# Attention scores of a two-layer decoder: one PSUM bank per head, and the keys' low parts multiplied by the queries' high parts alone in half of the array's rows

## The chip, the core and the metric

The kernel runs on one core of a Trainium2 chip. The core has five engines with an instruction queue each: TensorE (PE in the profile, its weight loads PEld), VectorE (DVE), ScalarE (ACT), GpSimd (POOL) and SyncE (SP, which here only issues DMAs). TensorE multiplies a stationary operand, loaded into its 128x128 array, with a moving operand, and writes to PSUM, which has eight banks; DVE and ACT read PSUM, POOL does not. The metric is the device time of one execution in microseconds (us).

## What is computed

The reference has two layers on x of 256 positions by 2048 channels: a retention and short-convolution mixer, then sliding-window attention. The change touches the attention scores of the second layer alone:

```python
def swa_sinks(q, k, v, sinks):          # 32 query heads, 4 key heads, head width 64
    ...                                 # blocks of 128 queries, n = 2 blocks
    scores = jnp.einsum('bnihgd,bnjhd->bnhgij', qb, kk) * (d ** -0.5)
    band = (kj <= qi) & (qi - kj < WINDOW)           # WINDOW = 128
    scores = jnp.where(valid, scores, -1e30)
    m = jnp.maximum(jnp.max(scores, axis=-1, keepdims=True), sink)
    p = jnp.exp(scores - m)
    p = p / (jnp.sum(p, axis=-1, keepdims=True) + jnp.exp(sink - m))
    return jnp.einsum('bnhgij,bnjhd->bnihgd', p, vv)
```

Query block 0 sees key block 0 under a causal mask. Query block 1 sees, for each key position, either the key of block 0 or the one of block 1: the window is exactly one block long, so of the two products at one position just one is valid, and the kernel picks between them by a triangular mask.

## The kernel before

**Products in three terms.** Every fp32 matrix is split into a high part (rounded to the type that TensorE reads at full rate, fp32r) and a low part, the rest. The four big projections are computed as high x high + high x low + low x high. Weights come in pieces of 512 KB (`Chunk.split`, L156): a DMA, an ACT copy that rounds to the high part (`wh`, L164), a DVE subtraction that leaves the low part (`wl`, L165). A piece feeds 12 matmuls of 128x128 by 128x512 (L142); `wh` and `wl` have five buffers each. Eight pieces make a chunk of 512 output columns.

**Small work between the pieces.** Attention is a generator that is advanced one step after each piece (`feed` calls `step`, L131 to 135), so that its small matmuls stand between the 12 matmuls of one piece and those of the next. The odd layer's chunks alternate queries and gates (`ODD_KIND`), for four groups g of eight heads, one key head each. The instructions go to each engine's queue in an order that a scheduler makes from the program; every engine then works through its queue strictly in that order.

**A group's steps.** `turn_q` transposes the rotated queries into `qT` (names q1T in the profile): for a pair of heads, the even head's high part stands in partitions 0 to 63 and its low part in 64 to 127, the odd head's the other way round. `kT` holds the keys twice, in both halves of the partitions, as high parts (index 0) and low parts (index 1). Then `scores(j, h)` (L608) is called four times per group, j = 0, 1 and h = 0, 2, each time for two heads: 16 calls in all. After two calls `shift(j)` (L630) makes the exponents' offsets `nm` and the sinks' terms `es`; `exponentials` (L645) takes the exponential of a 128x128 tile per head and query block on ACT, in place in `pr`, summing into `den`; `turn_p` (L677) transposes four such tiles into a PSUM tile `pt`, which ACT copies to `ph` (L685) and DVE subtracts into `pl` (L686); `turn_gate` (L667) transposes the gate into `gt`; `values` multiplies with the values into `ov`.

**PSUM.** The pool `at` has two banks, for score tiles and `ov` in turn, and `tp` has two banks, for all transposes (`pt`, `gt`, `qt`) in turn. A tile can be written only when the readers of the tile two before it in its pool are done.

**One call of scores before.** Six matmuls with 256 moving columns each: for each head of the pair one for query block 0 (L613, moving operand: high and low keys of block 0 side by side, into the first bank) and two for query block 1 (L615 with the high keys of both blocks, L616 with the low ones, added up in the second bank). The stationary operand has 128 rows, high and low parts of the query, so all four products are formed, low x low as well. ACT copies the first half of bank one for both heads (L618), DVE adds the other half (L619), adds the mask and takes the maximum per head (L621); ACT copies half of bank two (L626), DVE overwrites the places of the other key block by `copy_predicated` (L627) and takes maxima (L628).

Of the kernel before, what the change touches and what calls it, by code (L numbers as in the profile page):

```python
# [8 lines left out]
F32 = mybir.dt.float32  # L9
F32R = mybir.dt.float32r  # L10
AF = mybir.ActivationFunctionType
ALU = mybir.AluOpType
# [3 lines left out]
P = 128  # L16
D = 2048
S = 256
# [7 lines left out]
HD = 64  # L26
# [13 lines left out]
C_AMASK = C_ID + 128  # L40
C_LOWER = C_AMASK + P
# [16 lines left out]
def hybrid_kernel(  # L58
# [13 lines left out]
    nc = tc.nc  # L72
# [7 lines left out]
    at = ctx.enter_context(tc.tile_pool(name="at", bufs=2, space=PSUM))  # L80

    cst = cp.tile([P, C_END], F32, tag="cst", name="cst")
# [383 lines left out]
    op = ctx.enter_context(tc.tile_pool(name="o", bufs=1))  # L466
# [21 lines left out]
    kT = op.tile([P, 4, T, 2, P], F32R, tag="kT", name="kT")  # L488
# [1 line left out]

    vs = op.tile([P, 3, 4, 2, HD], F32R, tag="vs", name="vs")
    act2 = Act("a2")
    lower = cst[:, C_LOWER : C_LOWER + P].bitcast(mybir.dt.uint32).unsqueeze(1).broadcast_to([P, 2, P])

    def work(name, shape, dt=F32):
        return tw.tile(shape, dt, tag="w2", name=name)
# [89 lines left out]
    def attention(g, rr, rs, qs):  # L586
        ah, al = act2.new()
        qT = op2.tile([P, 4, 2, T, P], F32R, tag="qT", name=f"q1T{g}", bufs=1)
# [18 lines left out]

        def scores(j, h):  # L608

            s0 = at.tile([P, 2, 2, P], F32, tag="at", name=f"s0{g}{j}{h}")  # L610
            s1 = at.tile([P, 2, S], F32, tag="at", name=f"s1{g}{j}{h}")
            for i in range(2):
                nc.tensor.matmul(s0[:, i], qT[:, 2 * j + h // 2, i, 0, :], kT[:, g, 0], start=True, stop=True)  # L613
            for i in range(2):
                nc.tensor.matmul(s1[:, i], qT[:, 2 * j + h // 2, i, 1, :], kT[:, g, :, 0, :], start=True, stop=False)  # L615
                nc.tensor.matmul(s1[:, i], qT[:, 2 * j + h // 2, i, 1, :], kT[:, g, :, 1, :], start=False, stop=True)  # L616
            p0, p1 = pr[j][:, h : h + 2, 0, :], pr[j][:, h : h + 2, 1, :]
            nc.scalar.activation(p0, s0[:, :, 0, :], AF.Copy)  # L618
            nc.vector.tensor_tensor(out=p0, in0=s0[:, :, 1, :], in1=p0, op=ALU.add)  # L619
            for i in range(2):  # L620
                nc.vector.tensor_tensor_reduce(  # L621
                    out=p0[:, i], in0=p0[:, i], in1=cst[:, C_AMASK : C_AMASK + P], scale=1.0, scalar=-3.0e38,
                    op0=ALU.add, op1=ALU.max, accum_out=mx[j][:, 0, h + i : h + i + 1],
                )

            nc.scalar.activation(p1, s1[:, :, 0:P], AF.Copy)  # L626
            nc.vector.copy_predicated(p1, lower, s1[:, :, P:S])  # L627
            nc.vector.tensor_reduce(out=mx[j][:, 1, h : h + 2], in_=p1, axis=AX.X, op=ALU.max)  # L628

        def shift(j):  # L630
# [88 lines left out]
        for t in range(T):  # L719
            nc.vector.tensor_scalar(  # L720
                out=rr[:, t, :], in0=rs[t], scalar1=r1[:, t : t + 1], scalar2=HD ** -0.5, op0=ALU.mult, op1=ALU.mult
# [9 lines left out]
        for j in range(2):  # L731
            mx[j] = op2.tile([P, T, 4], F32, tag="mx", name=f"mx{g}{j}")
            pr[j] = op2.tile([P, 4, T, P], F32, tag="pr", name=f"pr{g}{j}")
            scores(j, 0)
            if j:
                exponentials(0, 0)
            yield
            scores(j, 2)
            shift(j)
            if j:  # L740
                exponentials(0, 1)
                divisor(0)
            yield
# [72 lines left out]
    for t in range(T):  # L816
# [3 lines left out]
        for c in range(1 + t):  # L820
            n = slice(c * N // (1 + t), (c + 1) * N // (1 + t))
# [84 lines left out]
```

## Time and profile before

| what | value |
|---|---|
| runs shown, median (lowest to highest) | 794.79 us (793.71 to 795.48), 3 runs |
| profiled execution, its own time | 795.05 us |
| its span, first to last instruction | 793.1 us |
| busy share PE, DVE, ACT, POOL | 99%, 64%, 52%, 6% |
| calls of scores in the span | 16, from 534.6 to 704.7 us |
| matmuls of scores | 96, of 3620 |

The busy share of an engine is an average over the span. A matmul's duration in the records holds its way through the array, so the pace of PE is read from the starts of successive instructions rather than from durations. Times of rows are microseconds from the span's start. A row of the timeline gives start, length, engine, line, operation, output and inputs, shapes and how often; a bracket tells how long the engine was idle before and who ended that.

### The profile page before, as it was taken

The page shows a single profiled execution, that of the slowest core. Times are in us where ns is not written, and L with a number is a line of the kernel's source. Part 1 is how long each engine was busy: PE and PEld are TensorE (multiplying, and loading weights), DVE is VectorE, ACT ScalarE, POOL GpSimd, SP SyncE. Part 2 cuts the span into 40 slices and gives each one's busy share as a digit, 9 for nine tenths or more (in the row PEclk, how much of TensorE's full clock was granted, in tenths as well). Part 3 has the DMA queues.
Part 4 walks back from the last instruction along what each step waited for, and adds up shares of the span by engine and source line. Part 5 has one row for each costly group of instructions (what it writes and reads, how often), then busy time and mean ns, then how long its engine had stood idle before and what let it go on. Part 6 is the DMA issues. An engine that isn't in the chain of part 4 may idle for free.

```text
span 793.1 us, 9901 instructions
## 1 busy us (share of the span) xinstructions
PE 786.6 (99%) x3620; PEld 651.5 (82%) x3620; DVE 505.9 (64%) x759; ACT 414.1 (52%) x645; POOL 45.0 (6%) x45
## 2 busy tenths in 40 slices
PE   8999999999999999999999999999999999999998
PEld 6888888888888888888888888888888888888886
DVE  6666454664445466545857664797998887977651
ACT  6743434444443434343435444658758678686431
POOL 0000000000000000000000000210300301301000
PEclk9999999999999999999999999999999999999999
DMA  8966645555456555556555555463464464445750
GB/s 311 394 241 230 201 145 186 184 183 191 134 188 201 194 185 186 187 186 206 167 198 172 186 186 189 156 213 107 159 213 130 140 209 159 156 138 185 233 166 26
DMA packets 41375, 147.09 MB, mean 185 GB/s; under 512 B 4720, under 2 KB 5360, under 8 KB 41072
## 3 DMA queue, kind: packets, MB, share of 16 engines
q1 hardware_dynamic: 40896, 146.21, 55.0%
q8 instruction: 28, 0.46, 0.2%
q10 hardware_dynamic: 432, 0.27, 0.1%
q14 instruction: 19, 0.16, 0.1%
HBM read 144.36 MB, written 2.10 MB: 185 GB/s over the span
## 4 chain that ended last, share of the span: by engine, by line
PE 99%; DMA 1%; ACT 0%; DVE 0%; ACTq 0%; DVEq 0%; issue 0%
PE pse L142 44%; PE psoq L142 11%; PE psoo L142 11%; PE psog L142 11%; PE pseo L142 11%; PE psokv L142 3%; PE pt L681 1%; PE ov L704 1%; PE ov L703 1%; DMA xt<-in_xt 1%; PE s L613 0%; PE s L616 0%; PE s L615 0%; PE gt L672 0%; PE qt L598 0%; PE rt L284 0%
## 5 line engine op out<-in xcount | busy, mean ns | idle before, releaser
L165 DVE TENSOR_TENSOR wle<-we,whe 128x1024 fp32r<-128x1024 f32 (+1 forms) x129 | 156.4, 1217 | 147.9 <-ACT whe L164 147.7
L164 ACT ACTIVATE whe<-we 128x1024 fp32r<-128x1024 f32 (+1 forms) x129 | 135.4, 1052 | 173.1 <-PE pse L142 158.8
L142 PE MATMUL pse<-whe,a0h 128*128 128x512 f32 x512 | 200.1, 396 | 1.3 <-ACT whe L164 1.3
L142 PE MATMUL pse<-whe,a0l 128*128 128x512 f32 x512 | 198.4, 391 | 0.0
L142 PE MATMUL pse<-wle,a0h 128*128 128x512 f32 x512 | 197.6, 390 | 0.0
L142 PEld LDWEIGHTS pse<-whe,a0h 128*128 128x128 f32 x512 | 96.6, 189 | 22.4 <-ACT whe L164 2.9
L142 PEld LDWEIGHTS pse<-whe,a0l 128*128 128x128 f32 x512 | 96.7, 189 | 20.3
L142 PEld LDWEIGHTS pse<-wle,a0h 128*128 128x128 f32 x512 | 96.3, 188 | 19.5
L164 ACT ACTIVATE wheo<-weo 128x1024 fp32r<-128x1024 f32 x32 | 33.9, 1061 | 48.2 <-PE pseo L142 32.7
L165 DVE TENSOR_TENSOR wleo<-weo,wheo 128x1024 fp32r<-128x1024 f32 x32 | 39.2, 1225 | 27.5 <-ACT wheo L164 27.5
L164 ACT ACTIVATE whoo<-woo 128x1024 fp32r<-128x1024 f32 x32 | 33.9, 1062 | 40.3 <-PE psoo L142 32.7
L165 DVE TENSOR_TENSOR wloo<-woo,whoo 128x1024 fp32r<-128x1024 f32 x32 | 38.9, 1224 | 24.8 <-ACT whoo L164 24.4
L164 ACT ACTIVATE whoq<-woq 128x1024 fp32r<-128x1024 f32 x32 | 34.0, 1062 | 35.3 <-PE psoq L142 14.3
L142 PE MATMUL psog<-whog,a1h 128*128 128x512 f32 x128 | 51.1, 400 | 0.0
L142 PE MATMUL psoq<-whoq,a1h 128*128 128x512 f32 x128 | 50.9, 398 | 0.0
L142 PE MATMUL pseo<-wheo,c0h 128*128 128x512 f32 x128 | 50.8, 397 | 0.0
L142 PE MATMUL psoo<-whoo,a2h 128*128 128x512 f32 x128 | 50.3, 393 | 0.0
L142 PE MATMUL psoo<-whoo,a2l 128*128 128x512 f32 x128 | 50.1, 391 | 0.0
L142 PE MATMUL psog<-whog,a1l 128*128 128x512 f32 x128 | 50.0, 391 | 0.0
L142 PE MATMUL psoq<-wloq,a1h 128*128 128x512 f32 x128 | 50.0, 391 | 0.0
L142 PE MATMUL psoq<-whoq,a1l 128*128 128x512 f32 x128 | 50.0, 391 | 0.0
L142 PE MATMUL pseo<-wheo,c0l 128*128 128x512 f32 x128 | 50.0, 391 | 0.0
(177 smaller groups left out, 1209.4 us busy)
## 6 DMA issues: line engine op xcount, KB each, us to landing
we<-in_w SPq DMA_DIRECT2D x127, 512.0 KB, 3.3
weo<-in_w SPq DMA_DIRECT2D x32, 512.0 KB, 3.3
woq<-in_w SPq DMA_DIRECT2D x32, 512.0 KB, 4.4
wog<-in_w SPq DMA_DIRECT2D x32, 512.0 KB, 3.3
woo<-in_w SPq DMA_DIRECT2D x32, 512.0 KB, 4.3
wokv<-in_w SPq DMA_DIRECT2D x8, 512.0 KB, 3.3
x<-in_xr SPq DMA_DIRECT2D x2, 1024.0 KB, 8.5
out_y<-y SPq DMA_DIRECT2D x7, 256.0 KB, 4.2
```

The source lines that it names most:

```text
L142: nc.tensor.matmul(self.ps[t], self.act(kt)[a][:, t * P : (t + 1) * P], w[:, k * N : (k + 1) * N], start=self.n[t] == 1, stop=self.n[t] == ...
L164: nc.scalar.activation(wh[:, ws], raw[:, ws], AF.Copy)
L165: nc.vector.tensor_tensor(out=wl[:, ws], in0=raw[:, ws], in1=f32(wh[:, ws]), op=ALU.subtract)
L681: nc.tensor.transpose(tr[:, h, :], pr[j][:, h, t, :], ident)
L703: nc.tensor.matmul(of, v, ph, start=first, stop=False)
L704: nc.tensor.matmul(of, v, pl, start=False, stop=last)
```

## The change

`scores` is rewritten. Each head of the pair has a bank of its own, `sc[i]`, with three blocks of 128 columns: block 0 for query block 0, blocks 1 and 2 for query block 1 against the two key blocks. Per head, two matmuls use all 128 rows (high and low queries by high keys: 128 and 256 moving columns, L615). Then four matmuls add the low keys, and they take only the 64 partitions that hold the head's high queries, 0 to 63 for the even head and 64 to 127 for the odd one, alternating (128, 128, 256, 256 columns, L622). The product of low queries with low keys is left out. The ACT copy and the DVE addition of query block 0 go; the mask and maximum read PSUM directly (L628); the ACT copy and the predicated copy of query block 1 are now one per head (L634, L635).

```diff
-    lower = cst[...].bitcast(mybir.dt.uint32).unsqueeze(1).broadcast_to([P, 2, P])
+    lower = cst[...].bitcast(mybir.dt.uint32)
...
-            s0 = at.tile([P, 2, 2, P], F32, tag="at", name=f"s0{g}{j}{h}")
-            s1 = at.tile([P, 2, S], F32, tag="at", name=f"s1{g}{j}{h}")
+            sc = [at.tile([P, 3, P], F32, tag="at", name=f"s{g}{j}{h}{i}") for i in range(2)]
             for i in range(2):
-                nc.tensor.matmul(s0[:, i], qT[:, 2 * j + h // 2, i, 0, :], kT[:, g, 0], start=True, stop=True)
-            for i in range(2):
-                nc.tensor.matmul(s1[:, i], qT[:, 2 * j + h // 2, i, 1, :], kT[:, g, :, 0, :], start=True, stop=False)
-                nc.tensor.matmul(s1[:, i], qT[:, 2 * j + h // 2, i, 1, :], kT[:, g, :, 1, :], start=False, stop=True)
+                for t, n in ((0, slice(0, 1)), (1, slice(1, 3))):
+                    k = kT[:, g, : t + 1, 0, :]
+                    nc.tensor.matmul(
+                        sc[i][:, n], qT[:, 2 * j + h // 2, i, t, :], k, start=t == 0, stop=False, skip_group_check=True
+                    )
+
+            for t, n in ((0, slice(0, 1)), (1, slice(1, 3))):
+                for i in range(2):
+                    e = slice(i * HD, (i + 1) * HD)
+                    nc.tensor.matmul(
+                        sc[i][:, n], qT[e, 2 * j + h // 2, i, t, :], kT[e, g, : t + 1, 1, :],
+                        start=False, stop=True, skip_group_check=True,
+                    )
-            nc.scalar.activation(p0, s0[:, :, 0, :], AF.Copy)
-            nc.vector.tensor_tensor(out=p0, in0=s0[:, :, 1, :], in1=p0, op=ALU.add)
             for i in range(2):
                 nc.vector.tensor_tensor_reduce(
-                    out=p0[:, i], in0=p0[:, i], in1=cst[:, C_AMASK : C_AMASK + P], ...
+                    out=p0[:, i], in0=sc[i][:, 0], in1=cst[:, C_AMASK : C_AMASK + P], ...
                 )
-            nc.scalar.activation(p1, s1[:, :, 0:P], AF.Copy)
-            nc.vector.copy_predicated(p1, lower, s1[:, :, P:S])
+            for i in range(2):
+                nc.scalar.activation(p1[:, i], sc[i][:, 1], AF.Copy)
+                nc.vector.copy_predicated(p1[:, i], lower, sc[i][:, 2])
```

Lines behind `scores` stand eight further down in the changed file (the exponentials are L648 before and L656 now, `pl` is L686 before and L694 now).

The queues change with it, beyond `scores` itself. First **PE, the fourth call of group 1**, before (s_4798 and s_4799 are the call's two score tiles, q1T the queries):

```order
L142 MATMUL psoq_1_4699<-whoq_2_4781,a1l_3201 128x512
L613 MATMUL s_4798<-kT,q1T_4563 128x256 x2
L615 MATMUL s_4799<-kT,q1T_4563 128x256
L616 MATMUL s_4799<-kT,q1T_4563 128x256
L615 MATMUL s_4799<-kT,q1T_4563 128x256
L616 MATMUL s_4799<-kT,q1T_4563 128x256
```

and now:

```order
L142 MATMUL psoq_1_4709<-whoq_2_4795,a1l_3201 128x512
L615 MATMUL s_4812<-kT,q1T_4571 128x128
L615 MATMUL s_4812<-kT,q1T_4571 128x256
L615 MATMUL s_4813<-kT,q1T_4571 128x128
L615 MATMUL s_4813<-kT,q1T_4571 128x256
L622 MATMUL s_4812<-kT,q1T_4571 128x128
L622 MATMUL s_4813<-kT,q1T_4571 128x128
L622 MATMUL s_4812<-kT,q1T_4571 128x256
L622 MATMUL s_4813<-kT,q1T_4571 128x256
```

Six matmuls become eight at the same place; the first needs the first bank and the third needs the second bank, where before the first two needed one bank and the next four the other.

Then **ACT, from the third call of group 1 to behind the fourth**, before (L618 and L626 copy score tiles, L648 are exponentials of the first two calls' scores, L643 the sinks' exponential, L164 the rounding of a weight piece):

```order
L164 ACTIVATE whoq_6_4935<-woq_6_4934 128x1024
L643 ACTIVATE es_4734<-es_4734 128x8
L618 ACTIVATE pr_4760<-s_4761 128x2x128
L626 ACTIVATE pr_4760<-s_4762 128x2x128
L648 ACTIVATE pr_4677,den_4735<-pr_4677,nm_4733,rr_4457 128x128 x5
L618 ACTIVATE pr_4760<-s_4798 128x2x128
L626 ACTIVATE pr_4760<-s_4799 128x2x128
L648 ACTIVATE pr_4677,den_4735<-pr_4677,nm_4733,rr_4457 128x128 x3
L164 ACTIVATE whoq_7_4965<-woq_7_4964 128x1024
```

and now (L634 are the copies, L656 the exponentials):

```order
L164 ACTIVATE whoq_6_4951<-woq_6_4950 128x1024
L651 ACTIVATE es_4746<-es_4746 128x8
L656 ACTIVATE pr_4685,den_4747<-pr_4685,nm_4745,rr_4465 128x128 x4
L634 ACTIVATE pr_4772<-s_4773 128x128
L634 ACTIVATE pr_4772<-s_4774 128x128
L656 ACTIVATE pr_4685,den_4747<-pr_4685,nm_4745,rr_4465 128x128 x4
L164 ACTIVATE whoq_7_4981<-woq_7_4980 128x1024
L634 ACTIVATE pr_4772<-s_4812 128x128
```

Four exponentials now stand ahead of the third call's copies, and the other four and a weight piece ahead of the fourth call's. Groups 2 and 3 have the same rows; in group 0 one exponential stands ahead of the third call's copies.

Last **DVE, behind the fourth call of group 1**, before (L165 are weight pieces, pl_4854 is the low part of the first transposed tile pt_4848):

```order
L663 TENSOR_TENSOR gv_4693<-gv_4693,den_4735 128x2x256
L165 TENSOR_TENSOR wloq_7_4966<-woq_7_4964,whoq_7_4965 128x1024
L686 TENSOR_TENSOR pl_4854<-pt_4848,ph_4853 128x512
L686 TENSOR_TENSOR pl_4886<-pt_4880,ph_4885 128x512
L655 TENSOR_TENSOR den_4815<-den_4815,es_4814 128x8
```

and now (L635 are the fourth call's predicated copies, L636 its maxima, L647 to L650 `shift`, pl_4870 the low part of the first transposed tile):

```order
L165 TENSOR_TENSOR wloq_7_4982<-woq_7_4980,whoq_7_4981 128x1024
L635 COPY_PREDICATED pr_4772<-cst,s_4812 128x128
L635 COPY_PREDICATED pr_4772<-cst,s_4813 128x128
L671 TENSOR_TENSOR gv_4703<-gv_4703,den_4747 128x2x256
L636 TENSOR_REDUCE mx_4771<-pr_4772 128x2
L647 TENSOR_TENSOR mx_4771<-mx_4771,rr_4465 128x8
L648 TENSOR_TENSOR mx_4771<-mx_4771,sml 128x8
L165 TENSOR_TENSOR wlog_0_5061<-wog_0_5059,whog_0_5060 128x1024
L649 TENSOR_SCALAR nm_4829<-mx_4771 128x8
L650 TENSOR_TENSOR es_4830<-sml,mx_4771 128x8
L694 TENSOR_TENSOR pl_4870<-pt_4864,ph_4869 128x512
```

The first low part `pl` stood right behind the piece wloq_7; now the fourth call's copies and maxima, the gate's scaling and the next piece wlog_0 stand between the two. Groups 2 and 3 again have the same rows; in group 0 `pl` still follows wloq_7.

More of the change, by code (lines that the diff above doesn't have):

```diff
@@ L492, in hybrid_kernel @@
     act2 = Act("a2")
-    lower = cst[:, C_LOWER : C_LOWER + P].bitcast(mybir.dt.uint32).unsqueeze(1).broadcast_to([P, 2, P])
+    lower = cst[:, C_LOWER : C_LOWER + P].bitcast(mybir.dt.uint32)
     def work(name, shape, dt=F32):
@@ L608, in scores @@
         def scores(j, h):
-            s0 = at.tile([P, 2, 2, P], F32, tag="at", name=f"s0{g}{j}{h}")
-            s1 = at.tile([P, 2, S], F32, tag="at", name=f"s1{g}{j}{h}")
+            sc = [at.tile([P, 3, P], F32, tag="at", name=f"s{g}{j}{h}{i}") for i in range(2)]
             for i in range(2):
-                nc.tensor.matmul(s0[:, i], qT[:, 2 * j + h // 2, i, 0, :], kT[:, g, 0], start=True, stop=True)
-            for i in range(2):
-                nc.tensor.matmul(s1[:, i], qT[:, 2 * j + h // 2, i, 1, :], kT[:, g, :, 0, :], start=True, stop=False)
-                nc.tensor.matmul(s1[:, i], qT[:, 2 * j + h // 2, i, 1, :], kT[:, g, :, 1, :], start=False, stop=True)
+                for t, n in ((0, slice(0, 1)), (1, slice(1, 3))):
[10 more added lines that the diff above has]
+                    )
             p0, p1 = pr[j][:, h : h + 2, 0, :], pr[j][:, h : h + 2, 1, :]
-            nc.scalar.activation(p0, s0[:, :, 0, :], AF.Copy)
-            nc.vector.tensor_tensor(out=p0, in0=s0[:, :, 1, :], in1=p0, op=ALU.add)
             for i in range(2):
                 nc.vector.tensor_tensor_reduce(
-                    out=p0[:, i], in0=p0[:, i], in1=cst[:, C_AMASK : C_AMASK + P], scale=1.0, scalar=-3.0e38,
+                    out=p0[:, i], in0=sc[i][:, 0], in1=cst[:, C_AMASK : C_AMASK + P], scale=1.0, scalar=-3.0e38,
                     op0=ALU.add, op1=ALU.max, accum_out=mx[j][:, 0, h + i : h + i + 1],
                 )
-            nc.scalar.activation(p1, s1[:, :, 0:P], AF.Copy)
-            nc.vector.copy_predicated(p1, lower, s1[:, :, P:S])
+            for i in range(2):
+                nc.scalar.activation(p1[:, i], sc[i][:, 1], AF.Copy)
+                nc.vector.copy_predicated(p1[:, i], lower, sc[i][:, 2])
             nc.vector.tensor_reduce(out=mx[j][:, 1, h : h + 2], in_=p1, axis=AX.X, op=ALU.max)
```

## The prediction

> **What bounds the kernel now.** I read the busy shares first, then the chain that ended last, then PE's list of waits.
>
> ```profile
> PE 786.6 (99%) x3620; PEld 651.5 (82%) x3620; DVE 505.9 (64%) x759; ACT 414.1 (52%) x645; POOL 45.0 (6%) x45
> ...
> PE 99%; DMA 1%; ACT 0%; DVE 0%; ACTq 0%; DVEq 0%; issue 0%
> ...
> PE warm L199 <- DVE zero L196: 1.5, 1, 1.5
> PE pse L142 <- ACT whe L164: 1.3, 1, 1.3
> ```
>
> PE is busy for 99% of the span, is 99% of the chain, and its matmuls waited only twice, both times at the program's start. So the end is set by the pace of PE's queue: whatever lengthens one of its rows, or makes one of its rows wait, is paid in full, and work taken from DVE or ACT is worth nothing by itself. PE's pace at the fourth call of group 1 and behind it:
>
> ```profile
> 597.90 0.39 PE L142 MATMUL psoq<-whoq,a1l 128*128 128x512 f32 x1
> 598.13 0.40 PE L613 MATMUL s<-kT,q1T 128*128 128x256 f32 x2
> 598.36 0.28 PE L615 MATMUL s<-kT,q1T 128*128 128x256 f32 x1
> 598.48 0.28 PE L616 MATMUL s<-kT,q1T 128*128 128x256 f32 x1
> 598.60 0.28 PE L615 MATMUL s<-kT,q1T 128*128 128x256 f32 x1
> 598.72 0.28 PE L616 MATMUL s<-kT,q1T 128*128 128x256 f32 x1
> 598.84 0.40 PE L142 MATMUL psoq<-whoq,a1h 128*128 128x512 f32 x1
> ...
> 601.59 0.60 PE L681 MATMUL pt<-cst,pr 128*128 128x128 f32 x4
> ...
> 604.80 0.60 PE L681 MATMUL pt<-cst,pr 128*128 128x128 f32 x4
> 605.24 0.60 PE L672 MATMUL gt<-cst,gv 128*128 128x128 f32 x4
> ```
>
> From start to start a 512-column matmul takes 0.23 us (597.90 to 598.13) and a 256-column one 0.12. A call takes 598.84 - 598.13 = 0.71, the 12 matmuls behind it 2.75, and the next call is due 3.46 after the last.
>
> **Term one: the call's own length on PE.** Six rows of 256 columns go, eight come: four with all rows of the array (128, 256, 128, 256 columns), four with half of the rows (128, 128, 256, 256). The trace has no fp32r matmul of 128 columns, none in half the rows, and no two that ran side by side. The nearest rows are the retention's:
>
> ```profile
> 100.58 0.63 PEld L299 LDWEIGHTS rsc<-qT,kT 128*128 128x128 f32 x4
> ...
> 100.79 0.61 PE L299 MATMUL rsc<-qT,kT 128*128 128x128 f32 x4
> 101.24 1.03 PE L295 MATMUL rsc<-qT,kT 128*128 128x256 f32 x4
> ```
>
> Four 128-column matmuls with a weight load each took 101.24 - 100.79 = 0.45, so 0.11 each; that is fp32, which streams slower, so it is the upper end. The lower end is the line through 0.23 and 0.12, which gives 0.07. The four full rows then take between 2 x 0.07 + 2 x 0.12 = 0.38 and 0.46. The four half rows take 0.19 if the two heads' halves run side by side, and up to 0.46 if they run in turn. Without a price for going from full to half rows and back the call lies between 0.56 and 0.92. For that price no row exists. Nothing speaks for a gain from it, so its lower end is zero; the upper end is an empty array and a load that is not hidden: 0.28 - 0.12 = 0.16 of tail (598.36 row) plus a 0.19 load (PEld rows below), 0.35 per switch, 0.70 per call. So a call takes 0.56 to 1.62. I take 0.92, no overlap and no price of switching: it is the row nearest to what runs here, since in the L299 rows, as in all, a matmul with its own load never starts less than 0.11 after the last. That is +0.21 per call, 16 x 0.21 = **+3.4 us**.
>
> A rule speaks against this choice: the Trainium skill, "TensorE: Matmul & The Clock Gate", section "Part 3: Packing small matmuls — row/col tiling", says that matmuls in different row groups of the array run at the same time, the next starting some 4 ns after the last. By that rule the half rows take 0.19, the call 0.65, and term one would be 16 x -0.06 = -1 us. No row of before shows two matmuls at once, so it stays a rival.
>
> **Term two: PE waits for its two banks at the fourth call.** The call's tiles take the two banks of the third call. What frees a bank is now the predicated copy, which needs the ACT copy of the same head. Before, group 1:
>
> ```profile
> 594.87 1.06 ACT L164 ACTIVATE whoq<-woq 128x1024 fp32r<-128x1024 f32 x1 [1.85 <-PE psoq L142]
> 595.85 0.21 ACT L643 ACTIVATE es<-es 128x8 f32<-128x8 f32 x1
> 595.97 0.37 ACT L618 ACTIVATE pr<-s 128x256 f32<-128x256 f32 x1
> 596.23 0.38 ACT L626 ACTIVATE pr<-s 128x256 f32<-128x256 f32 x1
> 596.49 0.49 ACT L648 ACTIVATE pr<-pr,nm,rr 128x128 f32<-128x128 f32 x1
> ...
> 596.97 0.49 ACT L648 ACTIVATE pr<-pr,nm,rr 128x128 f32<-128x128 f32 x1
> ...
> 595.96 1.23 DVE L165 TENSOR_TENSOR wloq<-woq,whoq 128x1024 fp32r<-128x1024 f32 x1
> 597.11 0.42 DVE L619 TENSOR_TENSOR pr<-s,pr 128x256 f32<-128x256 f32 x1
> 597.44 0.44 DVE L627 COPY_PREDICATED pr<-cst,s 128x256 f32<-128x256 uint32 x1
> 597.77 0.28 DVE L621 CUSTOM_DVE_ANT_0 pr<-pr,cst 128x128 f32<-128x128 f32 x1
> ...
> 597.98 0.29 DVE L621 CUSTOM_DVE_ANT_0 pr<-pr,cst 128x128 f32<-128x128 f32 x1
> 598.19 0.42 DVE L628 TENSOR_REDUCE mx<-pr 128x2 f32<-128x256 f32 x1
> ```
>
> The rounding at 594.87 is released by PE and keeps its place. Now four exponentials follow `es` at once, 0.48 apart (596.49 to 596.97), from 595.97 to 597.89, and only then the copies: 0.27 each (0.37 less 128 columns), the first ends at 598.16. DVE, done with the maxima by then, copies 598.20 to 598.50 (0.30, by 0.44 less 128 columns). What PE makes of a bank that is late is seen once, in group 0:
>
> ```profile
> 544.61 0.42 DVE L619 TENSOR_TENSOR pr<-s,pr 128x256 f32<-128x256 f32 x1 [0.57 <-ACT pr L618]
> ...
> 544.76 0.39 PE L142 MATMUL psoq<-whoq,a1l 128*128 128x512 f32 x1
> 545.09 0.50 PE L613 MATMUL s<-kT,q1T 128*128 128x256 f32 x2
> ...
> 545.09 0.30 PEld L613 LDWEIGHTS s<-kT,q1T 128*128 128x128 f32 x2 [0.37 <-DVE pr L619]
> 545.32 0.19 PEld L142 LDWEIGHTS psoq<-whoq,a1h 128*128 128x128 f32 x1
> ```
>
> The addition ended at 545.03, the load began at 545.09, and the pair took 0.50 where it takes 0.40: matmuls flow 0.16 after the release. So the fourth call starts at 598.66. Due was 598.13, plus 0.21 by the longer third call: **a wait of 0.32**. The longer a call, the shorter this wait, since ACT and DVE count from the start of the third call. In group 0 one exponential is ahead: copy to 544.97, bank free at 545.31, start 545.47, due 544.99 + 0.21: 0.27, against 0.20 paid there before, so +0.06.
>
> **Term three: PE waits at the gate's transposes.** `gt` takes the `tp` bank of the first `pt`, which is free after `pl`. ACT goes on with four exponentials to 600.15 and the piece's rounding to 601.21. DVE does the same piece, 1.23, to 602.47, two predicated copies to 602.9, and then what is listed in the changed queue; the gate's scaling, the small steps of `shift` and `pl` are sized by these rows:
>
> ```profile
> 595.18 0.17 DVE L639 TENSOR_TENSOR mx<-mx,rr 128x8 f32<-128x8 f32 x1
> 595.38 0.17 DVE L640 TENSOR_TENSOR mx<-mx,sml 128x8 f32<-128x8 f32 x1
> ...
> 601.62 0.69 DVE L663 TENSOR_TENSOR gv<-gv,den 128x512 f32<-128x512 f32 x1
> 602.23 1.22 DVE L165 TENSOR_TENSOR wloq<-woq,whoq 128x1024 fp32r<-128x1024 f32 x1
> 603.37 0.68 DVE L686 TENSOR_TENSOR pl<-pt,ph 128x512 fp32r<-128x512 f32 x1
> ```
>
> Scaling to 603.49, maxima (0.42) to 603.83, two small steps to 604.24, the next piece to 605.38, two small steps, `pl` 605.47 to 606.16. Before, `pl` ended at 604.05, 1.2 ahead of `gt`. PE, from 598.66: call 0.92, 12 matmuls 2.75, from `pt` to `pt` 3.21 (601.59 to 604.80), four transposes 0.44: `gt` is due at 605.98 and starts at 606.16 + 0.16 = 606.32, **a wait of 0.34**. Group 0 has `pl` right behind the piece and no such wait.
>
> The saved DVE addition and ACT copy hide nothing: those engines' time was covered by PE's. At the second call a weight piece also stands ahead of the predicated copies now:
>
> ```profile
> 589.28 0.42 DVE L619 TENSOR_TENSOR pr<-s,pr 128x256 f32<-128x256 f32 x1
> ```
>
> From 589.28, where DVE reaches the first call's tiles, two maxima of 0.21, the piece (1.15 to the next start) and a copy of 0.30 end at 591.15, so matmuls flow at 591.31. That call was due at 598.13 - 2 x 3.46 = 591.21; a first call longer by 0.21 covers it, one of 0.56 would make it 0.25.
>
> **The sum.** 3.4 + 3 x (0.32 + 0.34) + 0.06 = 5.4. From the profiled execution, 795.05 (its span of 793.1 and 1.95 around it), 800.5; the runs' median lies 0.26 below that execution, so **800.2 us**.
>
> **Rivals.**
>
> *The array empties at each switch.* Nothing in the trace shows full and half rows next to each other. With the 0.16 of tail at both switches a call takes 1.24: 16 x 0.53 = 8.5, the waits are covered, and the 0.20 of group 0 goes: 8.3, so 803.1. With loads exposed as well, 16 x 0.91 = 14.6: up to 809. The Trainium skill, "TensorEngine Tiling (Array Packing)", section "Tiling Modes", says that a change of tiling mode drains TensorE; by that rule this is the case, and no row of before shows it.
>
> *The halves overlap, and the waits eat the gain.* A call of 0.56 saves 16 x 0.15 = 2.4, but banks do not come earlier: in groups 1 to 3 the fourth call waits 0.68, `gt` 0.70, the second call 0.25, so a group loses 1.63 - 0.60 = 1.03, group 0 0.08; together 3.2, so 798.0. For it speaks that neighbouring half rows share neither rows nor bank; against it that all starts in the trace are in turn. By the rule on row groups above this is the case.
>
> *Faster.* The same overlap, with banks that are free when PE arrives: 795.05 - 2.4 - 0.26 = 792.4. It decides only if ACT and DVE free the third call's first bank by 597.8, 0.7 ahead of my walk; four exponentials of 0.48 stand against that.
>
> *No change.* The half rows do not do what the text says and cost what the old rows cost (0.71 a call), and half of the waits arise: at most +1.6.
>
> **Chances.** Forecast 0.50 (its own range 798.5 to 802.5), emptying array 0.22, overlap eaten 0.13, no change 0.09, faster 0.06. A measurement of this kernel can tell about 0.2%, 1.6 us, from no change. Faster 0.06, within 0.2% 0.09, slower 0.85. The range of 8 in 10 leaves out the faster case, most of the unchanged one and the top of the emptying one: 796.5 to 806.
>
> **What would show it.** Starts within a call: L622 rows of one pair closer than 0.1 us mean overlap; a gap ahead of the first L622 or of the next L142 means a price of switching. PEld's wait ahead of the fourth call's first L615, on DVE L635, about 0.3 us in groups 1 to 3, shows term two; PEld's wait at L680 on DVE L694 shows term three. Should calls be at 0.56 and neither wait exist, I am wrong in both halves; waits of more than 0.6 with short calls are the second rival.

## The result, and the profile after

| | before | changed |
|---|---|---|
| median of the runs, us | 794.93 | 801.34 |
| range of the runs, us | 793.71 to 795.48 | 800.59 to 802.08 |
| the profiled execution, us | 795.05 | 801.4 |
| its span, us | 793.1 | 799.5 |

The ratio is 1.0085, with an interval of 1.0073 to 1.0097: by the medians, the change makes the kernel 6.4 us slower. The forecast of 800.2 lies 1.1 us below that, and its range of 796.5 to 806 holds it. The page of the changed kernel, its busy times and its chain of work:

```profile
PE 792.9 (99%) x3652; PEld 652.5 (82%) x3652; DVE 502.7 (63%) x759; ACT 412.3 (52%) x645; POOL 45.0 (6%) x45
...
PE 99%; DMA 1%; ACT 0%; DVE 0%; ACTq 0%; DVEq 0%; issue 0%
```

PE still sets the end. DVE and ACT have 3.2 and 1.8 us less to do, and that buys nothing. The timeline of the changed kernel, first PE and then its weight loads, around the second call of group 1 (start, duration, engine, line, tiles, shape, number of instructions):

```profile
592.75 0.39 PE L142 MATMUL psoq<-whoq,a1l 128*128 128x512 f32 x1
592.98 0.62 PE L615 MATMUL s<-kT,q1T 128*128 128x128 f32 x4
593.53 0.49 PE L622 MATMUL s<-kT,q1T 64*128 64x128 f32 x4
593.96 0.50 PE L142 MATMUL psoq<-whoq,a1h 128*128 128x512 f32 x1
594.29 0.39 PE L142 MATMUL psoq<-wloq,a1h 128*128 128x512 f32 x1
...
592.76 0.64 PEld L615 LDWEIGHTS s<-kT,q1T 128*128 128x128 f32 x4
593.53 0.30 PEld L622 LDWEIGHTS s<-kT,q1T 64*128 64x128 f32 x4
593.95 0.19 PEld L142 LDWEIGHTS psoq<-whoq,a1h 128*128 128x128 f32 x1
594.06 0.19 PEld L142 LDWEIGHTS psoq<-wloq,a1h 128*128 128x128 f32 x1
```

Three things are to be seen.

- **Overlap.** The four half-row loads take 0.30: one is 0.19, so they come two at a time, the second pair 0.11 behind the first. Four in turn would take 0.19 + 3 x 0.11 = 0.52, and the run with both heads in one half, below, shows just that.
- **Late loads.** The first L622 load starts with its matmul (both 593.53), and so does the load of the first L142 behind the call (593.95 and 593.96). Elsewhere the load starts while the matmul ahead is at work: that of the first L615 at 592.76, 0.22 early.
- **A slow step behind the call.** From the first L142 to the second it is 594.29 - 593.96 = 0.33 where 0.23 is usual.

For all kernels below, the length of a call is taken from its first row to the second L142 row behind it, less one L142 step of 0.23; so that slow step counts. Here it is 594.29 - 592.98 - 0.23 = **1.08**. In the kernel before the slow step does not exist and the call is 0.71. That is +0.37 for each of 16 calls, 5.9 of the 6.4 us.

The fourth call of group 1, in the timeline of the changed kernel, PE and then PEld:

```profile
600.39 0.39 PE L142 MATMUL psoq<-whoq,a1l 128*128 128x512 f32 x1
600.65 0.72 PE L615 MATMUL s<-kT,q1T 128*128 128x128 f32 x4
...
602.07 0.40 PE L142 MATMUL psoq<-wloq,a1h 128*128 128x512 f32 x1
...
600.65 0.53 PEld L615 LDWEIGHTS s<-kT,q1T 128*128 128x128 f32 x4 [0.29 <-DVE pr L635]
```

The load waits for the predicated copy L635 as forecast. The call starts 0.03 late (600.65 - 600.39 = 0.26) and is 602.07 - 600.65 - 0.23 = 1.19 long, 0.11 over the others: a wait of 0.14, not 0.32. In the list of waits this line has four entries of at most 0.3, and no wait at L680 is listed.

### The profile page after: what moved, and what is told of

Same layout as the page of the kernel before. It is cut to its first block, busy times and chain, and to the rows that moved or that the text cites. A ratio compares the mean times of both kernels' runs of the same rounds, so it can differ in the third digit from the quotient of the medians.

```text
span 799.5 us, 9957 instructions
## 1 busy us (share of the span) xinstructions
PE 792.9 (99%) x3652; PEld 652.5 (82%) x3652; DVE 502.7 (63%) x759; ACT 412.3 (52%) x645; POOL 45.0 (6%) x45
## 4 chain that ended last, share of the span: by engine, by line
PE 99%; DMA 1%; ACT 0%; DVE 0%; ACTq 0%; DVEq 0%; issue 0%
PE pse L142 44%; PE psoq L142 11%; PE psoo L142 11%; PE psog L142 11%; PE pseo L142 11%; PE psokv L142 3%; PE s L615 1%; PE pt L689 1%; PE s L622 1%; PE ov L712 1%; PE ov L711 1%; DMA xt<-in_xt 1%; PE gt L680 0%; PE rt L284 0%; PE qt L598 0%; PE x1t L447 0%
## 5 line engine op out<-in xcount | busy, mean ns | idle before, releaser
L165 DVE TENSOR_TENSOR wle<-we,whe 128x1024 fp32r<-128x1024 f32 (+1 forms) x129 | 156.4, 1216 | 148.1 <-ACT whe L164 147.7
L164 ACT ACTIVATE whe<-we 128x1024 fp32r<-128x1024 f32 (+1 forms) x129 | 135.5, 1053 | 174.5 <-PE pse L142 160.1
L142 PE MATMUL pse<-whe,a0h 128*128 128x512 f32 x512 | 199.8, 395 | 1.4 <-ACT whe L164 1.4
L142 PE MATMUL pse<-whe,a0l 128*128 128x512 f32 x512 | 198.1, 391 | 0.0
L142 PE MATMUL pse<-wle,a0h 128*128 128x512 f32 x512 | 197.3, 389 | 0.0
L142 PEld LDWEIGHTS pse<-whe,a0h 128*128 128x128 f32 x512 | 96.6, 189 | 22.5 <-ACT whe L164 3.0
L142 PEld LDWEIGHTS pse<-whe,a0l 128*128 128x128 f32 x512 | 96.7, 189 | 20.4
L142 PEld LDWEIGHTS pse<-wle,a0h 128*128 128x128 f32 x512 | 96.2, 188 | 19.5
L164 ACT ACTIVATE wheo<-weo 128x1024 fp32r<-128x1024 f32 x32 | 33.9, 1061 | 48.2 <-PE pseo L142 32.7
L165 DVE TENSOR_TENSOR wleo<-weo,wheo 128x1024 fp32r<-128x1024 f32 x32 | 39.2, 1224 | 27.5 <-ACT wheo L164 27.5
L165 DVE TENSOR_TENSOR wloo<-woo,whoo 128x1024 fp32r<-128x1024 f32 x32 | 39.1, 1224 | 24.8 <-ACT whoo L164 24.6
L164 ACT ACTIVATE whoo<-woo 128x1024 fp32r<-128x1024 f32 x32 | 33.8, 1060 | 39.8 <-PE psoo L142 31.7
L142 PE MATMUL psoq<-whoq,a1h 128*128 128x512 f32 x128 | 52.1, 407 | 0.0
L164 ACT ACTIVATE whoq<-woq 128x1024 fp32r<-128x1024 f32 x32 | 33.9, 1059 | 33.4 <-PE psoq L142 12.4
L142 PE MATMUL psog<-whog,a1h 128*128 128x512 f32 x128 | 51.1, 399 | 0.0
L142 PE MATMUL psoo<-whoo,a2h 128*128 128x512 f32 x128 | 50.7, 396 | 0.0
L142 PE MATMUL pseo<-wheo,c0h 128*128 128x512 f32 x128 | 50.7, 396 | 0.0
L142 PE MATMUL psoo<-whoo,a2l 128*128 128x512 f32 x128 | 50.0, 391 | 0.0
L142 PE MATMUL psoq<-whoq,a1l 128*128 128x512 f32 x128 | 50.0, 391 | 0.0
L142 PE MATMUL psog<-whog,a1l 128*128 128x512 f32 x128 | 50.0, 390 | 0.0
L142 PE MATMUL pseo<-wheo,c0l 128*128 128x512 f32 x128 | 49.9, 390 | 0.0
L142 PE MATMUL psoq<-wloq,a1h 128*128 128x512 f32 x128 | 49.9, 390 | 0.0
```

What stands on the lines that cost most here:

```text
L142: nc.tensor.matmul(self.ps[t], self.act(kt)[a][:, t * P : (t + 1) * P], w[:, k * N : (k + 1) * N], start=self.n[t] == 1, stop=self.n[t] == ...
L164: nc.scalar.activation(wh[:, ws], raw[:, ws], AF.Copy)
L165: nc.vector.tensor_tensor(out=wl[:, ws], in0=raw[:, ws], in1=f32(wh[:, ws]), op=ALU.subtract)
```

## The experiments

Each ran beside the kernel before on the same chip; ratios are to that. The first four were sent with one theory, called D: half-row pairs overlap fully, and each change between full and half rows empties the array (0.155) and then shows a weight load (0.108). The starts of the records suggested these sizes.

One thing moves the totals that no edit touches. All queues are the same in all kernels up to the first call, and yet the profiled executions reach it between 533.15 and 535.28 us: the program's first eight weight matmuls take 10.05 - 6.68 = 3.37 us in the kernel before, and 8.42 - 6.41 = 2.01 in the run with one half-row matmul. The head-order run and the run with the banks alone begin like the latter; what decides it was not followed. So call lengths, and the stretch from the first call to the end of the span, tell more than totals. That stretch is 793.1 - 534.6 = 258.5 before and 799.5 - 534.6 = 264.9 in the changed kernel.

### All 128 rows for the low keys

```diff
-                    e = slice(i * HD, (i + 1) * HD)
                     nc.tensor.matmul(
-                        sc[i][:, n], qT[e, 2 * j + h // 2, i, t, :], kT[e, g, : t + 1, 1, :],
+                        sc[i][:, n], qT[:, 2 * j + h // 2, i, t, :], kT[:, g, : t + 1, 1, :],
```

> The changed kernel with the four matmuls of L622 over all 128 rows instead of 64, so the low parts of the queries times the low parts of the keys are added again; banks, order and copies as changed. No half-row matmuls are left, so nothing switches. Theory D (a change between full and half rows empties the array, 0.155, and then shows a weight load, 0.108, together 0.263 and twice a call; the half-row pairs themselves overlap): eight matmuls at about 0.115, call 0.92 instead of the 1.08 of the changed kernel, 16 x 0.16 = 2.6 us less, of which waits at the fourth call and at `gt` take back up to 2: 799 to 801, with span 0.5 to 2.6 below the changed kernel's. Rival 1 (eight loads and matmuls instead of six are the price, whatever their rows): call 1.08 as in the changed kernel, time 801.3. Rival 3 (the copies in one bank per head and the waits behind them are the price): call length falls, the time stays at 801.3 by waits of the same size.

Measured: 799.3 us, ratio 1.0053 (1.0037 to 1.007), span 797.8. The timeline, the second call of group 1 with its second group of loads, then the fourth call with its wait:

```profile
592.10 0.62 PE L615 MATMUL s<-kT,q1T 128*128 128x128 f32 x4
592.56 0.62 PE L621 MATMUL s<-kT,q1T 128*128 128x128 f32 x4
593.02 0.40 PE L142 MATMUL psoq<-whoq,a1h 128*128 128x512 f32 x1
593.25 0.40 PE L142 MATMUL psoq<-wloq,a1h 128*128 128x512 f32 x1
...
592.44 0.53 PEld L621 LDWEIGHTS s<-kT,q1T 128*128 128x128 f32 x4
...
599.19 0.39 PE L142 MATMUL psoq<-whoq,a1l 128*128 128x512 f32 x1
599.63 0.72 PE L615 MATMUL s<-kT,q1T 128*128 128x128 f32 x4
...
600.89 0.40 PE L142 MATMUL psoq<-wloq,a1h 128*128 128x512 f32 x1
...
599.63 0.52 PEld L615 LDWEIGHTS s<-kT,q1T 128*128 128x128 f32 x4 [0.47 <-DVE pr L634]
```

The call is 593.25 - 592.10 - 0.23 = 0.92: eight steps of 0.115, though half of the matmuls have 128 columns and half 256. So behind another load a 128-column matmul costs a full load step; its stream alone would be a quarter of L142's 0.23. For 256 columns the stream, half of 0.23, is as long as the step, and the two can't be told apart here. The loads now take 0.53 for four, one after another. With more arithmetic than the changed kernel the call is shorter by 0.16: eight instructions as such are not the price, and rival 1 falls. What makes the changed kernel's call longer than this one is in the half rows or in getting there.

The fourth call waits 0.21 ahead of its first row (599.63 - 599.19 = 0.44) and is 1.03 long, so 0.32 in all.

### The half-row matmuls twice

```diff
-            for t, n in ((0, slice(0, 1)), (1, slice(1, 3))):
+            for t, n in 2 * ((0, slice(0, 1)), (1, slice(1, 3))):
                 for i in range(2):
                     e = slice(i * HD, (i + 1) * HD)
```

> The changed kernel with the four half-row matmuls of L622 issued twice in a row, so that the queries' high parts times the keys' low parts are added twice; twelve matmuls a call, still two changes of rows. Theory D (pairs overlap, 0.263 a change of rows): a second half part without a change is 0.057 + 0.107 = 0.164, call 1.08 -> 1.25, 16 x 0.164 = +2.6 us over the changed kernel, about 803.5 to 804. Rival 2 (half-row matmuls as such show their loads, 0.42 to 0.43 for four): call 1.51, +6.7 us, about 808. Rival 1 (each load and matmul has its pitch, 1.08 / 8 = 0.136): four more are +0.54 a call, +8.6 us, about 810.

Measured: 809.85 us, ratio 1.0186 (1.0171 to 1.0201), span 808.1. The time matches rival 1 and the call does not. The timeline, and then three lines of the list of waits (engine, tile and line, what it waited for, sum, number, longest):

```profile
590.89 0.62 PE L615 MATMUL s<-kT,q1T 128*128 128x128 f32 x4
591.44 0.72 PE L622 MATMUL s<-kT,q1T 64*128 64x128 f32 x8
...
592.43 0.39 PE L142 MATMUL psoq<-wloq,a1h 128*128 128x512 f32 x1
...
591.44 0.53 PEld L622 LDWEIGHTS s<-kT,q1T 64*128 64x128 f32 x8
```

```profile
PE gt L680 <- DVE pl L694: 1.8, 4, 0.5
...
PE pt L689 <- DVE pl L694: 0.7, 3, 0.2
...
PEld s L615 <- DVE pr L635: 2.0, 7, 0.5
```

The call is 1.31, +0.23 for four more half-row matmuls. Theory D said 0.164, rivals 1 and 2 0.43 to 0.54. Eight half-row loads take 0.53, as long as four full ones above: a pair takes one load step, on the mean of the 128- and the 256-column pair 0.115. So the pairs do overlap, but theory D had the step too short. 16 x 0.23 = 3.7 of the 8.5 us over the changed kernel are calls. Most of the rest is waits: the scheduler put DVE's and ACT's work into another order here, and PE waits at L680 in every group and at L689 in three. The time of this run tells nothing by itself.

### Four changes of rows a call

```diff
-            for i in range(2):
-                for t, n in ((0, slice(0, 1)), (1, slice(1, 3))):
+            for t, n in ((0, slice(0, 1)), (1, slice(1, 3))):
+                for i in range(2):
                     k = kT[:, g, : t + 1, 0, :]
...
-            for t, n in ((0, slice(0, 1)), (1, slice(1, 3))):
                 for i in range(2):
                     e = slice(i * HD, (i + 1) * HD)
```

> The changed kernel with the same eight matmuls in another order: for each query block the two full-row ones and then the two half-row ones, so a call changes rows four times instead of twice; the same values are computed. Theory D: two more changes, 2 x 0.263 = +0.526, call 1.08 -> 1.6, 16 x 0.526 = 8.4 us, less the waits of about 0.15 at the four fourth calls which the longer calls cover: +7.8 to +8.4, about 809 to 810. Rivals 1 and 2 (number of loads, or half-row loads as such) and 3 (the waits): the same matmuls cost the same, call 1.08, about 801.

Measured: 806.08 us, ratio 1.0137 (1.0122 to 1.0152), span 804.2. The timeline of one call:

```profile
590.36 0.33 PE L616 MATMUL s<-kT,q1T 128*128 128x128 f32 x2
590.62 0.33 PE L621 MATMUL s<-kT,q1T 64*128 64x128 f32 x2
590.88 0.51 PE L616 MATMUL s<-kT,q1T 128*128 128x256 f32 x2
591.31 0.38 PE L621 MATMUL s<-kT,q1T 64*128 64x256 f32 x2
591.63 0.50 PE L142 MATMUL psoq<-whoq,a1h 128*128 128x512 f32 x1
591.97 0.40 PE L142 MATMUL psoq<-wloq,a1h 128*128 128x512 f32 x1
```

The same eight matmuls, with every other engine's queue in the same order as in the changed kernel, now take 591.97 - 590.36 - 0.23 = 1.38 a call, +0.30. Two more changes of rows cost that much, so neither the count of matmuls nor the waits are the price; the wait at the fourth call is gone altogether. Theory D was right in kind and too high in size: 4.7 us instead of 7.8.

### One half-row matmul in the kernel before

```diff
-                nc.tensor.matmul(s1[:, i], qT[:, 2 * j + h // 2, i, 1, :], kT[:, g, :, 1, :], start=False, stop=True)
+                e = slice(HD, P) if i else slice(0, P)
+                nc.tensor.matmul(s1[:, i], qT[e, 2 * j + h // 2, i, 1, :], kT[e, g, :, 1, :], start=False, stop=True)
```

> The kernel before with one edit: the last of the six matmuls of a call (second head, second query block, low parts of the keys) runs in rows 64 to 127 alone, which leaves out the low parts of the queries times the low parts of the keys for that head and block. Six matmuls, banks, copies and queues as before. Theory D: five full-row matmuls, a change, one half-row one, a change back: about 5 x 0.116 + 0.263 + 0.107 + 0.263 = 1.21 against 0.73, so +0.49 a call, 16 x 0.49 = +7.8 us, about 802.7, as slow as the changed kernel by one matmul of it. Rivals 1 and 3 (two more loads; banks and waits): nothing is added, call 0.73, time as before, 795. Rival 2 (a half-row matmul shows its own load, about 0.1): +1.7 us, 796.6.

Measured: 800.65 us, ratio 1.0072 (1.0057 to 1.0087), span 798.7. One call in the timeline, the last matmul being the edited one:

```profile
588.20 0.40 PE L613 MATMUL s<-kT,q1T 128*128 128x256 f32 x2
588.43 0.28 PE L615 MATMUL s<-kT,q1T 128*128 128x256 f32 x1
588.55 0.28 PE L617 MATMUL s<-kT,q1T 128*128 128x256 f32 x1
588.67 0.28 PE L615 MATMUL s<-kT,q1T 128*128 128x256 f32 x1
588.88 0.38 PE L617 MATMUL s<-kT,q1T 64*128 64x256 f32 x1
589.19 0.50 PE L142 MATMUL psoq<-whoq,a1h 128*128 128x512 f32 x1
589.53 0.40 PE L142 MATMUL psoq<-wloq,a1h 128*128 128x512 f32 x1
```

This isolates the price. One matmul of six in half the rows, nothing else touched, and the kernel is 5.4 us slower by the medians, nearly as slow as by the whole change; from the first call to the end it takes 798.7 - 533.6 = 265.1, against 264.9 in the changed kernel. The call is 1.10, +0.39 for two changes, so **about 0.20 for one**. How it is made up shows here without overlap. The last full matmul starts at 588.67 and streams 256 columns, about half of L142's 0.23; the half-row one starts 0.21 later, so some 0.10 pass with nothing streaming. Behind it the step from L142 to L142 is 0.34 instead of 0.23: 0.11 for a load that nothing covers. Each change has both parts: from the half-row matmul to the first L142 it takes 0.31, which is such a load of 0.11, a stream of some 0.11 and again 0.09 with nothing streaming. Of the sizes that theory D had, 0.108 was right, and 0.155 was too long: it was counted from the recorded start of the last L615, whose own load had not ended by then.

What is left of theory D has two parts: **a load step is 0.115, and two loads in different halves of the rows share one; a change between full and half rows is 0.20.** These two sizes come from the run with all rows and from this one. By them the call of the changed kernel is 4 + 2 steps and two changes, 0.69 + 0.40 = 1.09, against 1.08. Eight steps and two changes, 0.92 + 0.40 = 1.32, are what half rows twice took (1.31), and, further down, both heads in one half (1.31). The call with four changes comes out too long, 0.69 + 0.80 = 1.49 against 1.38: its two 128-column groups stand directly ahead of a change, where no further load fills the step, and each ends after its stream of some 0.06. The rows of that run show the difference: from the 128-column half rows to the next kind it takes 0.26 (590.62 to 590.88), from the 256-column ones 0.32 (591.31 to 591.63).

### The half rows in the order of heads

```diff
-            for t, n in ((0, slice(0, 1)), (1, slice(1, 3))):
-                for i in range(2):
+            for i in range(2):
+                for t, n in ((0, slice(0, 1)), (1, slice(1, 3))):
                     e = slice(i * HD, (i + 1) * HD)
```

> The changed kernel with the four half-row matmuls of a call in the order of heads: first head's two, then second head's two, instead of the heads in turn; the same values are computed. What the first four runs left of theory D: every weight load takes a slot of about 0.115, two loads in different halves of the rows share one slot, and each change between full and half rows costs about 0.205 (0.10 empty, 0.108 for a load that nothing covers). Then two loads in a row in the same half take a slot each, and only the second and the third matmul, neighbours in different halves, share one: three slots instead of two, call 1.08 -> 1.19, +1.8 us, about 803. Rival (two halves overlap wherever they stand, as if each half had a queue): call 1.08, about 801. Rival (what shares a slot is the pair that starts a stretch): four slots, call 1.30, +3.5 us. The queues of VectorE and ScalarE come out in another order here, so the length of the call decides, and the time may be off by the waits.

Measured: 800.64 us, ratio 1.0076 (1.0061 to 1.0091), span 797.8. PE's queue now has, at the half-row part of a call, the first head (`s_4123`) and then the second (`s_4124`):

```
 L622 MATMUL s_4123<-kT,q1T_4010 128x128
 L622 MATMUL s_4123<-kT,q1T_4010 128x256
 L622 MATMUL s_4124<-kT,q1T_4010 128x128
 L622 MATMUL s_4124<-kT,q1T_4010 128x256
```

The timeline, once over the whole call and once (last row) over 0.1 us alone:

```profile
591.57 0.62 PE L615 MATMUL s<-kT,q1T 128*128 128x128 f32 x4
592.12 0.50 PE L622 MATMUL s<-kT,q1T 64*128 64x128 f32 x4
...
592.88 0.39 PE L142 MATMUL psoq<-wloq,a1h 128*128 128x512 f32 x1
...
592.12 0.33 PE L622 MATMUL s<-kT,q1T 64*128 64x128 f32 x2
```

The call is 1.08 as before the edit: my three slots were wrong and the first rival was right. The last row says why. Both 128-column matmuls start within 0.1 us, and both 256-column ones later, though in the queue a 256-column one stands between the two of 128. The second head's matmul starts ahead of the first head's second. Each half of the rows works through its own part of the queue. So the sentence ahead of the prediction, that every engine works through its queue strictly in order, does not hold for the starts of matmuls in different halves. The 0.7 us that this run's median lies below the changed kernel's is not from the calls: from the first call to the end it takes 797.8 - 533.2 = 264.6, against 264.9.

### Rows 0 to 63, and one half alone

The one half-row matmul in the kernel before, moved to the first rows (the edit is against that run):

```diff
-                e = slice(HD, P) if i else slice(0, P)
+                e = slice(0, HD) if i else slice(0, P)
```

> As the run with one half-row matmul a call, but in rows 0 to 63: the last matmul of a call takes the first 64 rows, so for the second head and second query block the low parts of the queries times the low parts of the keys are added and the high parts times the low parts are left out. Theory D: the price is for the change of the number of rows, wherever they lie: call 1.12, +5.4 us over before, about 800.6, as with rows 64 to 127. Rival (the price is for weights that start at row 64, and 64 rows from row 0 are like 128): call 0.73, time of before, 795.

Measured: 800.29 us, ratio 1.0068 (1.0051 to 1.0085); call 1.10. Where the rows lie does not matter; their number does.

The changed kernel with both heads in the same half:

```diff
-                    e = slice(i * HD, (i + 1) * HD)
+                    e = slice(0, HD)
```

> The changed kernel with all four half-row matmuls of a call in rows 0 to 63; for the odd heads the low parts of the queries times the low parts of the keys are added and the high parts times the low parts are left out. Queues, banks and waits as changed. Theory D after the first seven runs (a weight load takes a slot of about 0.115, the two halves of the rows work through their matmuls side by side, a change between full and half rows costs about 0.205): with one half alone there is nothing to work beside, so four slots for four half-row matmuls instead of two, call 1.08 -> 1.30, +3.5 us less 0.6 of waits that the longer calls cover: 804 to 805. Rival (half-row matmuls are simply quick, whichever rows they use): call 1.08, 801.3.

Measured: 803.96 us, ratio 1.0107 (1.009 to 1.0124). The timeline of its loads in one call, and PE's rows for its length:

```profile
591.21 0.52 PEld L622 LDWEIGHTS s<-kT,q1T 64*128 64x128 f32 x4
...
590.66 0.62 PE L615 MATMUL s<-kT,q1T 128*128 128x128 f32 x4
...
592.20 0.39 PE L142 MATMUL psoq<-wloq,a1h 128*128 128x512 f32 x1
```

The four half-row loads take 0.52 where two halves take 0.30, and the call is 592.20 - 590.66 - 0.23 = 1.31. So the change's use of different halves is worth 0.23 a call; half-row matmuls as such are no quicker than full ones.

### The banks and the copies alone

The kernel before with a bank and copies per head, in part:

```diff
-            s0 = at.tile([P, 2, 2, P], F32, tag="at", name=f"s0{g}{j}{h}")
-            s1 = at.tile([P, 2, S], F32, tag="at", name=f"s1{g}{j}{h}")
+            sc = [at.tile([P, 4, P], F32, tag="at", name=f"s{g}{j}{h}{i}") for i in range(2)]
...
+            for i in range(2):
+                nc.scalar.activation(p0[:, i], sc[i][:, 0], AF.Copy)
+                nc.vector.tensor_tensor(out=p0[:, i], in0=sc[i][:, 1], in1=p0[:, i], op=ALU.add)
...
+                nc.scalar.activation(p1[:, i], sc[i][:, 2], AF.Copy)
+                nc.vector.copy_predicated(p1[:, i], lower, sc[i][:, 3])
```

> The kernel before with its six full-row matmuls a call, but a bank per head (first block's two products beside the second block's scores), and one copy, one add and one masked copy per head instead of per pair of heads; everything is computed as before. So this is the banks and the copies of the change without its matmuls. Theory D: six slots, call 0.73 as before; what is paid are waits at the fourth call, since the bank of the third call's first head is asked for as soon as PE comes to it: 0.33 at a call of 0.92, so about 0.5 at a call of 0.73, 4 x 0.5 less the 0.12 of before, +1.5 to +2, about 797. Rival 3 (banks and waits are most of the change's price): 800 or more. Rival (the smaller copies cost nothing): 795.

Measured: 795.64 us, ratio 1.0006 (0.9997 to 1.0016), span 792.1. The timeline:

```profile
586.37 0.40 PE L613 MATMUL s<-kT,q1T 128*128 128x256 f32 x2
586.61 0.64 PE L618 MATMUL s<-kT,q1T 128*128 128x256 f32 x4
587.09 0.40 PE L142 MATMUL psoq<-whoq,a1h 128*128 128x512 f32 x1
587.32 0.40 PE L142 MATMUL psoq<-wloq,a1h 128*128 128x512 f32 x1
```

The call is 0.72. A bank per head and copies per head cost at most 1.3 us by the interval, and some 0.5 from the first call to the end of this execution (792.1 - 533.15 = 259.0 against 258.5): rival 3 falls. My 797 was too high. The scheduler orders the queues differently for this kernel, and the waits fall elsewhere (0.13 at the third call, none at the fourth outside group 0). So it does not price the waits of the changed queues; those are read from the changed kernel itself, 0.14 at each fourth call.

## Why the prediction was right, and where its sizes were not

**The direction and the place were right.** PE paces the kernel, and a longer call on PE is most of the loss.

**Term one is the step that was mis-sized.** It said: "I take 0.92, no overlap and no price of switching". Both halves of that sentence are wrong. The halves overlap, which saves two load steps a call (1.31 when both heads use one half, against 1.08). Changing rows costs twice 0.20. The two errors partly cancel: 1.08 came out, so the term is 5.9 instead of 3.4. The run with all rows has neither half rows nor changes, and its call is 0.92, as the L299 rows gave it. So the row was well chosen for what it showed, eight loads in turn, and it could not show a change of rows.

The reason given for that choice, that a matmul with its own load never starts less than 0.11 after the last, holds for the mean of a stretch and not for single rows. In the kernel before, the L142 behind the gate's transposes starts 0.03 after the last of them (605.57 and 605.60); in the changed kernel an L615 of 256 columns starts 0.06 after the one of 128 ahead of it (592.98 and 593.04), both in full rows. So starts closer than 0.1, which the prediction named as the sign of overlap, don't settle it by themselves. The loads do, two at a time in 0.30 against 0.52, and the call length with them.

**The lower bound of 0.56 for overlap without a price was too low.** It took 128-column matmuls at 0.07. Behind another load they take a load step, 0.115, so six steps make about 0.69. Before, a call also has six steps. Even without any price of changing rows the change would have had about 0.02 a call to win, 0.3 us in all, by these numbers; no run shows that case.

**Term two had the right mechanism, for the call it assumed.** In the run whose call is 0.92 the fourth call waits 0.32 in group 1, the forecast number, and as much in group 0, where 0.27 was forecast. The text said that the wait shrinks as the call grows, and the runs with equal queues on DVE and ACT show it: 0.32 at 0.92, 0.14 at 1.08, none at 1.38.

**Term three was too large.** In the run whose call is 0.92, group 1:

```profile
606.62 0.60 PE L688 MATMUL pt<-cst,pr 128*128 128x128 f32 x4
607.20 0.66 PE L679 MATMUL gt<-cst,gv 128*128 128x128 f32 x4
607.61 0.47 PE L142 MATMUL psoq<-whoq,a1h 128*128 128x512 f32 x1
...
606.46 0.68 DVE L693 TENSOR_TENSOR pl<-pt,ph 128x512 fp32r<-128x512 f32 x1
```

The transposes start right behind the end of `pl`, as forecast. From the first `pt` to the L142 it takes 0.99, and 0.80 in the kernel before: a wait of some 0.2 in groups 1 to 3, none in group 0, where 0.34 in three was forecast. PE came there as late as the prediction had it. DVE was earlier by 0.08: from the release of the fourth call's bank to the start of `pl` it took 6.89 (599.57 to 606.46), where the walk had 605.47 - 598.50 = 6.97, by small parts of many steps. The rest is that the transposes followed the release by some 0.11 instead of the 0.16 of group 0's matmuls. In the changed kernel the longer calls bring PE to `gt` later still, and 0.03 is left of the wait in groups 1 and 2.

**The sum.** At the assumed call of 0.92 the forecast was 800.2, and the kernel that has that call took 799.3. The changed kernel: 16 x 0.37 = 5.9 for the calls, 4 x 0.14 for the waits less the 0.20 that group 0 paid before, 6.3 in all, against 6.4 of span. That 800.2 lies so near is in part luck: term one was 2.5 too small, and the two kinds of waits together were 1.6 too large.

**The rivals.** What happened is two of them at once. The array empties, as the Trainium skill's "TensorEngine Tiling (Array Packing)", section "Tiling Modes", says of a change of mode; it gives no price, and the runs put it at 0.20 with the load. That rival assumed halves in turn, and 0.35 for a change with its load. The halves overlap, as "TensorE: Matmul & The Clock Gate", section "Part 3: Packing small matmuls — row/col tiling", of the Trainium skill says: in the trace of the changed kernel the two matmuls of a pair start 2 to 6 ns apart, where the section has some 4. The same section says that matmuls start strictly in the order of the queue; the run in the order of heads shows otherwise across two halves.

**A version better than the kernel before** did not come out of this. All forms with half rows that ran have at least two changes a call, 0.40, and at least six load steps, as many as the kernel before has.

## What to carry to other kernels

Before splitting small matmuls into half rows, count weight-load steps and not columns: here a load and its matmul of up to 256 columns took 0.115 to 0.12 us on the mean of a stretch, and two in different halves share that. Each stretch of half-row work between full-row work pays 0.40 us, so it has to save four such steps; two heads of scores save two against full rows in turn. And where a bound is open because no row shows the case, look for which of two errors in the estimate can cancel: the forecast was near, but for a reason that did not hold.

## What the runs showed of the hardware

- A change between matmuls over 128 rows and over 64 rows costs 0.20 us each way: some 0.10 with nothing streaming, and a load of 0.11 that is not started while the other kind is at work. Rows 0 to 63 and 64 to 127 behave alike (call 1.10 for both).
- Matmuls in the two halves start out of the queue's order: 128-column ones 6 to 7 ns apart, with a 256-column one between them in the queue that started 0.16 later, in all 16 calls.
- A full-row fp32r matmul of 128 columns right behind another load takes as long as one of 256: eight of mixed widths take 0.92.
